# A 31-tap convolution as block-Toeplitz matmuls, LayerNorm sums on VectorE, and a mixer reordered by channel block, in a two-layer trunk on eight cores

## The chip, the cores and the metric

The kernel runs on the eight cores of one Trainium2 chip, two dies of four cores. Each core does the same work on its own 4096 tokens of 1024 channels. The metric is the device time of the slowest core. An execution falls into a fast state, or into a slow one in which the cores of one die, sometimes of both, show a lower granted TensorE clock and take longer. Stage times come from core 0 unless another core is named.

## The reference

Layer 0 is the part that changes. Its input projection feeds two mixers, whose outputs share one output projection:

```python
z = h @ w_in                                              # 1024 -> 2560
a_val, a_gate, b_gate, c_gate, b_val = jnp.split(z, [512, 1024, 1536, 2048], axis=-1)
a = a_val * jax.nn.sigmoid(a_gate)
a = causal_depthwise_conv(a, conv_a_w) + conv_a_b         # mixer A: 31 taps, 512 channels
a = jax.nn.silu(layer_norm(a, ln_a_g, ln_a_b))            # over the 512 channels
bo = b_gate * causal_depthwise_conv(c_gate * b_val, conv_b_w)   # mixer B: 3 taps
return jnp.concatenate([a, bo], axis=-1) @ w_out
```

A squared-ReLU MLP (1024 to 4096 and back) follows. Layer 1 has a chunked spatial gating mixer ("mixer 1" below) and another MLP. RMSNorm stands before each, and once more at the end.

## The kernel before

A core takes its tokens in four tiles of 1024 and runs mixer 0, MLP 0, mixer 1 and MLP 1 on each. The weights stream in pieces of 1 MB through a ring of four slots; GpSimd issues the next piece when TensorE has read an old one for the last time. SyncE issues everything else, in order.

Mixer A convolves with one diagonal matrix per tap and channel block; the matmuls use one entry in 128 of each matrix:

```python
for k in range(31):                       # for each of 4 blocks of 128 channels
    dg[j] = identf * w[:, k]              # built on VectorE
    e.matmul(banks[cb0], lhsT=dg[j], rhs=ab[:, k:k + 512], start=(k == 0), stop=(k == 30))
    e.matmul(banks[cb1], lhsT=dg[j], rhs=ab[:, 512 + k:1024 + k], ...)
```

LayerNorm's sums over channels are fp32 matmuls with a matrix of ones, 16 a tile. Mixer B then projects all c and v columns, and after them all b columns.

The last normalization multiplies into an output buffer, writes it out and loads the next tile's input behind it:

```python
small("dve", ... out=obuf[tb], in0=h[:, tb, :] ..., writes [("TT", "obuf", tb)])
P.op("sp", lambda e: e.dma_start(out=dst, in_=obuf[tb]), reads=[("TT", "obuf", tb)], dma="out")
if mt + 1 < n_mt:
    load_x(mt + 1, tb)
```

The name after `dma=` is the counter that the transfer increments. A later user of the same memory waits for that counter, and the helper always asks for its newest value, whichever transfer it was recorded for:

```python
if isinstance(s, tuple):       # a transfer's counter
    p = snap[s[1]]             # as many as have been issued by now
```

Between stages a "fence" folds all that is recorded for a memory region into one set, which every later write into the region waits for.

## Time and profile before

| what | us |
|---|---|
| three runs | 3658.84, 3241.15, 3693.83 |
| span of core 0 in the profiled run (fast) | 3245.0 |
| mixer 0 with its output projection, tiles 1 to 4 | 193.0, 194.2, 193.6, 191.2 |
| mixer 1, all tiles | 472.5 |
| both MLPs, all tiles | 1804.9 |
| before the first projection matmul | 44.5 |
| joints after tiles 1, 2, 3 | 30.0, 52.5, 50.8 |
| after the last matmul | 17.6 |

A stage begins with its first matmul and ends with the next stage's first; a joint runs from a tile's last matmul to the next tile's first projection matmul. The prediction below shows the views that this is read from.

### The profile page before, as it was taken

Reading aid. Unit: us, or ns where it says so; the run is one execution under the profiler, and the core shown is the slowest. Engines: PE = TensorE matmul, PEld = TensorE weight load, DVE = VectorE, ACT = ScalarE, POOL = GpSimd, SP = SyncE. Lnnn points to the kernel's source line nnn. Section 1 sums busy time; section 2 is a strip of 40 time slices with the busy share of each in tenths; the row PEclk is TensorE's granted clock in tenths of the full one; section 3 lists DMA queues with packets and bytes.
Section 4 is the critical chain, followed back from the end, with each engine's and each line's share of the span. In section 5 each row is a group of like instructions: output and inputs, shape, how many; then the busy total and the mean of one; then the engine's idle time right before and its main releaser. Section 6 shows DMA issues by size and latency. Waiting matters only on the chain.

```text
span 3245.0 us, 42214 instructions; the slowest of 8 cores (3232.0 to 3245.0 us)
## 1 busy us (share of the span) xinstructions
PE 2907.4 (90%) x13664; PEld 1346.0 (41%) x13936; DVE 1165.6 (36%) x2236; ACT 963.4 (30%) x1721; POOL 822.8 (25%) x865
## 2 busy tenths in 40 slices
PE   5989997999788999799779899979976989997997
PEld 3434443444334444344334344434433434443443
DVE  3461235313454214512245521451224452145123
ACT  2142145222223115521222411552122231155212
POOL 1004223342002331342200233134320023313432
PEclk9999998999899999899879999989987999998999
DMA  6235453466315453465811445335471144533542
GB/s 131 27 50 81 65 78 53 61 84 128 68 27 72 72 78 53 62 82 66 147 36 26 69 75 78 53 53 88 68 139 44 27 67 77 78 53 53 86 71 78
DMA packets 197205, 227.23 MB, mean 70 GB/s; under 512 B 3968, under 2 KB 188416, under 8 KB 196864
## 3 DMA queue, kind: packets, MB, share of 16 engines
q0 software_dynamic: 187200, 188.76, 41.1%
q1 hardware_dynamic: 9792, 35.76, 3.4%
q8 instruction: 118, 1.93, 0.2%
q14 instruction: 95, 0.78, 0.1%
HBM read 396.47 MB, written 16.78 MB: 127 GB/s over the span
## 4 chain that ended last, share of the span: by engine, by line
PE 76%; DVE 7%; issue 6%; DMA 5%; ACT 4%; POOL 1%; DVEq 0%; SPq 0%; ACTq 0%; POOLq 0%
PE bank L584 34%; PE bank L595 32%; PE bank L680 3%; PE bank L679 3%; DMA y<-TT 3%; PE bank L441 2%; DMA ring<-ev_w_out 1%; DVE TT L549 1%; POOL R L861 1%; DMA h<-x 1%; ACT R L810 1%; PE bank L707 1%; PE bank L700 1%; DVE TT L731 1%; ACT TT L806 1%
## 5 line engine op out<-in xcount | busy, mean ns | idle before, releaser
L584 PE MATMUL bank<-xnT,ring 128*128 128x512 bf16 x5756 | 1301.9, 385 | 57.3 <-ACT TT L756 22.1
L595 PE MATMUL bank<-ring,R 128*128 128x512 bf16 x5008 | 1132.0, 384 | 25.1 <-DVE R L782 11.2
L602 DVE TENSOR_TENSOR h<-bank,h 128x512 f32<-128x512 f32 x640 | 439.5, 691 | 1423.9 <-PE bank L595 1423.9
L584 PEld LDWEIGHTS bank<-xnT,ring 128*128 128x128 bf16 x5888 | 580.5, 99 | 767.8 <-issue 100.9
L595 PEld LDWEIGHTS bank<-ring,R 128*128 128x128 bf16 x5120 | 503.5, 99 | 627.0 <-issue 48.6
L621 ACT ACTIVATE TT<-bank 128x512 f32<-128x512 f32 x512 | 305.4, 597 | 1239.3 <-PE bank L584 1215.3
L623 POOL TENSOR_TENSOR R<-TT 128x512 bf16<-128x512 f32 x512 | 532.1, 1039 | 382.6 <-ACT TT L621 381.9
L441 PE MATMUL bank<-ident,xn_tm 128*128 128x128 bf16 x1024 | 90.4, 243 | 166.2 <-ACT st L454 98.9
L388 ACT ACTIVATE junk<-h 128x1024 bf16<-128x1024 f32 x160 | 167.0, 1044 | 134.3 <-DVE h L602 127.3
L679 PE MATMUL bank<-TT,dg 128*128 128x512 bf16 x480 | 181.2, 378 | 17.7 <-DVE dg L674 14.8
L680 PE MATMUL bank<-TT,dg 128*128 128x512 bf16 x496 | 188.5, 380 | 0.9
L298 POOL DMA_DIRECT2D ring<-w_0 x64 | 57.5, 898 | 444.9 <-PE bank L595 428.9
L298 POOL DMA_DIRECT2D ring<-w_1 x64 | 57.8, 903 | 441.4 <-PE bank L595 352.2
L426 ACT ACTIVATE xn_tm<-h,st 128x1024 bf16<-128x1024 f32 x112 | 128.2, 1144 | 127.6 <-DVE st L485 108.5
L444 DVE TENSOR_TENSOR xnT<-bank,sm 128x1024 bf16<-128x1024 bf16 x128 | 155.1, 1219 | 28.0 <-PE bank L441 26.7
L441 PEld LDWEIGHTS bank<-ident,xn_tm 128*128 128x128 bf16 x1024 | 74.6, 109 | 194.2 <-issue 178.1
L674 DVE TENSOR_SCALAR dg<-identf,sm 128x128 bf16<-128x128 f32 x496 | 133.7, 294 | 54.4 <-PE bank L680 5.0
L595 PE MATMUL bank<-ring,xnT 128*128 128x512 bf16 x500 | 114.3, 390 | 1.0 <-issue 0.4
L858 DVE TENSOR_TENSOR TT<-TT,biasT 128x512 f32<-128x512 f32 x64 | 71.7, 1154 | 80.0 <-ACT TT L849 76.7
L861 POOL TENSOR_TENSOR R<-TT,R 128x512 bf16<-128x512 f32 x64 | 95.9, 1532 | 8.2 <-ACT TT L849 5.2
L684 ACT ACTIVATE R<-bank,sm 128x512 f32<-128x512 f32 x32 | 22.0, 687 | 243.3 <-PE bank L680 241.8
L763 POOL COPY halo_c<-TT 128x2 f32<-128x2 f32 x16 | 6.0, 378 | 336.0 <-DVE TT L758 336.0
(84 smaller groups left out, 1159.3 us busy)
## 6 DMA issues: line engine op xcount, KB each, us to landing
ring<-w_0 POOLq DMA_DIRECT2D x64, 1024.0 KB, 11.5
ring<-w_1 POOLq DMA_DIRECT2D x64, 1024.0 KB, 11.9
ring<-ev_w_in POOLq DMA_DIRECT2D x20, 1024.0 KB, 14.0
h<-x SPq DMA_DIRECT2D x32, 512.0 KB, 7.1
ring<-od_w_in POOLq DMA_DIRECT2D x16, 1024.0 KB, 10.8
y<-TT SPq DMA_DIRECT2D x32, 512.0 KB, 3.7
ring<-ev_w_out POOLq DMA_DIRECT2D x8, 1024.0 KB, 13.6
ring<-od_w_out POOLq DMA_DIRECT2D x8, 1024.0 KB, 13.9
```

The costliest lines, as they stand in the source:

```text
L388: small("act", lambda e: e.activation(out=junk[jb][:], in_=h[:, tb, :], func=AF.Square, accum_out=st[:, c0 + tb:c0 + tb + 1]), h_keys(tb), ...
L441: r = e.transpose(tbk[:, kc * 128:(kc + 1) * 128], xn_tm[xb][:, kc * 128:(kc + 1) * 128], ident[:])
L444: small("dve", lambda e: e.tensor_tensor(out=xnT[:, :, tb * 128:(tb + 1) * 128], in0=tbk.rearrange("p (k n) -> p k n", k=8), in1=sm[:, SM_ ...
L584: r = e.matmul(banks[b][:], lhsT=ring[slot][:, kc, m * 128:(m + 1) * 128], rhs=xnT[:, kc, s * 512:(s + 1) * 512], start=(kc == 0), stop=(k ...
L595: r = e.matmul(banks[b][:], lhsT=lhs(kc, tb), rhs=ring[slot][:, kc, :], start=(kc == 0), stop=(kc == 7))
L602: small("dve", lambda e: e.tensor_tensor(out=h[:, tb, d * 512:(d + 1) * 512], in0=banks[b][:], in1=h[:, tb, d * 512:(d + 1) * 512], op=ALU ...
L621: small("act", lambda e, b=b, rb=rb: e.activation(out=rbuf[rb], in_=banks[b][:], func=AF.Relu), [("ps", b)], [("TT", "rbuf", rb)])
L623: small("pool", lambda e, rb=rb, hq=hq, c=j * 4 + m, s=s: e.tensor_tensor(out=hq[:, c, s * 512:(s + 1) * 512], in0=rbuf[rb], in1=rbuf[rb], ...
L674: small("dve", lambda e, j=j, m=m, k=k: e.tensor_scalar(out=dg[j][:], in0=identf[:], scalar1=sm[:, SM_CA + m * 31 + k:SM_CA + m * 31 + k + 1],
L679: e.matmul(banks[cb0][:], lhsT=dg[j][:], rhs=ab[:, k:k + 512], start=(k == 0), stop=(k == 30))
L680: return e.matmul(banks[cb1][:], lhsT=dg[j][:], rhs=ab[:, 512 + k:1024 + k], start=(k == 0), stop=(k == 30))
L861: small("pool", lambda e, hb=hb, sv3=sv3, tb=tb: e.tensor_tensor(out=yT[:, hb * 4:hb * 4 + 4, tb * 128:(tb + 1) * 128], in0=sv3, in1=uT[:, ...
```

## The change

The change means to take work from TensorE. Channels are cut into 16 groups of 32, and four token phases (token number modulo 4) are laid beside them, so that 128 rows hold 32 channels in four phases. One 128 by 128 block-Toeplitz matrix then does up to 16 products of tap and phase per channel, and nine lags replace 31 taps. The projection does not leave its result in that layout, so each block of 128 channels goes out to DRAM and comes back re-laid, and the normalized result goes through DRAM again on its way back ("hops"). The core of the diff:

```diff
-for k in range(31):                       # 248 matmuls of 512 columns a tile, 31 diagonals a block
-    dg[j] = identf * w[:, k]; matmul(cb0, dg[j], ab[:, k:k+512]); matmul(cb1, ...)
+for half_ in range(2):                    # 144 matmuls of 256 columns a tile, cw built once
+    g = 2 * gp + half_
+    for L in range(NLAG):                 # 9 lags
+        r = e.matmul(banks[b][:, half_ * TP:(half_ + 1) * TP], lhsT=cw[:, g, L * 128:(L + 1) * 128],
+                     rhs=A4.v[:, g, HB - L:HB - L + TP], start=(L == 0), stop=(L == NLAG - 1))
+# a_glu(m): the hop, on the sync queue
+P.op("sp", dma_start(out=scr_a[m] (4 phases), in_=ab), dma=f"a{m}")
+P.op("sp", dma_start(out=A4[4m:4m+4], in_=scr_a[m]), reads=[("scra", m)], dma=f"b{m}")
-mm1 / sums of squares: 16 fp32 matmuls with ones_f
+acc_s += pair; acc_q += pair * pair       # VectorE and ScalarE, under the convolution
+matmul(b, lhsT=blk, rhs=comb)             # one small matmul, within mixer B
+lazy(m, "pool", subtract mean); lazy(m, "dve", multiply by rstd); ScalarE Silu;
+lazy(m + 1, "sp", write scr_s[m]); lazy(m + 1, "sp", read back into mixT, two halves)
-mixer B: c and v columns of all blocks, then b columns of all blocks
+B_COLS = [c0, v0, c1, v1, b0, c2, v2, b1, c3, v3, b2, b3]; b_mix(m); b_gate(m - 1); b_release(min(m, 2))
-obuf: 8 buffers in region TT, all on counter "out", fenced between stages
+obuf: 4 buffers tracked by address, counters "out0" to "out3"
-x, y: rows tb * 128 to tb * 128 + 127 of a tile
+x, y: every fourth row of 512 (phase order)
-sm and cst loaded first, on counter "c"
+sm first, then x, then wexp and cst, all three on counter "c"
```

(The diff also moves the scratch tiles into one region tracked in steps of 256 bytes, and reorders the spatial weights to match the token order.)

## The prediction

> **Which time is meant.** The three runs before took 3658.84, 3241.15 and 3693.83 us: one fast, two slow. The profile fell in a fast run (its span is 3245.0 us), so I work from 3241 us and predict the fast state of the changed kernel.
>
> **What bounds the kernel now.** First the view of the cores, to know the state: both dies agree within 0.1%, so this is an undisturbed run.
>
> ```profile
> core 0: 3245.0 us, clock 0.957
> die 0 (median of its cores): 3236.5 us, clock 0.954
> die 1 (median of its cores): 3234.9 us, clock 0.958
> ```
>
> Next the page's chain of waits. TensorE is 76% of what ended last; the rest is not matmul, and that remainder is where waits hide. L584 and L595 are the plain projections, which the change leaves alone; L679 and L680 (the 31 taps) are 3% each; "DMA y<-TT 3%" is a surprise, since an output write should lie beside other work.
>
> ```profile
> PE 76%; DVE 7%; issue 6%; DMA 5%; ACT 4%; POOL 1%; DVEq 0%; SPq 0%; ACTq 0%; POOLq 0%
> PE bank L584 34%; PE bank L595 32%; PE bank L680 3%; PE bank L679 3%; DMA y<-TT 3%; PE bank L441 2%; DMA ring<-ev_w_out 1%; DVE TT L549 1%; POOL R L861 1%; DMA h<-x 1%; ACT R L810 1%; PE bank L707 1%; PE bank L700 1%; DVE TT L731 1%; ACT TT L806 1%
> ```
>
> Then I cut core 0 into stretches; the boundaries are where TensorE's line changes in the timeline. Each of the core's four tiles of 1024 tokens goes through the same stages. Tile 2's mixer 0 is three of the stretches below: mixer A with its convolution (837 to 926), the LayerNorm sums (926 to 941), and mixer B up to the start of the output projection (941 to 999). The row from 1322 is the spatial part of mixer 1. The last three are joints: the end of tile 1, the end of tile 2, and the end of the kernel. Read the length against PE busy.
>
> ```profile
> core 0: us, PE busy (x) PEld busy (x) DVE busy (x) ACT busy (x) POOL busy (x), PEclk, DMA share, GB/s
> 837.40:926.60 89.20, 82.66 (x368) 36.48 (x375) 39.86 (x133) 11.69 (x18) 3.51 (x10) 0.99 0.18 24
> 926.60:941.10 14.50, 14.45 (x32) 5.85 (x34) 2.08 (x3) 4.68 (x8) 0.00 (x0) 1.00 0.01 1
> 941.10:999.50 58.40, 47.41 (x197) 20.33 (x201) 43.70 (x52) 16.78 (x22) 5.32 (x10) 0.91 0.18 22
> 1322.30:1335.40 13.10, 5.53 (x65) 4.57 (x65) 10.62 (x13) 6.17 (x21) 10.20 (x8) 0.71 1.15 166
> 807.60:837.40 29.80, 8.10 (x64) 6.42 (x66) 18.12 (x37) 15.73 (x33) 1.08 (x2) 0.58 0.99 216
> 1598.60:1651.10 52.50, 8.13 (x66) 6.44 (x67) 21.96 (x45) 18.27 (x38) 1.00 (x2) 0.52 0.61 146
> 3213.00:3245.00 32.00, 14.31 (x65) 6.37 (x65) 15.74 (x30) 7.37 (x18) 0.00 (x0) 0.80 0.32 131
> ```
>
> Mixer A and the sums are bound by TensorE. Mixer B is not: its work is 192 matmuls, 41.5 us, in 58.4 us. And the joint after tile 2 costs 52.5 us where that after tile 1 costs 29.8.
>
> Last, the chain in time order, in mixer B, at the joint after tile 2, and at the end. TensorE sits before the output projection until the last piece of its weights lands; at the joint and at the end each final multiply waits for the output write before it.
>
> ```profile
> 986.79 12.34 DMA ring<-ev_w_out
> ```
>
> ```profile
> 1599.22 9.69 DMA y<-TT
> 1610.36 8.71 DMA y<-TT
> ```
>
> ```profile
> 3238.08 2.61 DMA y<-TT
> ```
>
> The source says why. All output writes share one counter, and the output buffers lie in a region that is fenced between stages, so after the first tile a write into any of them waits for every output write issued so far.
>
> The durations I use:
>
> ```profile
> L680 PE MATMUL bank<-TT,dg 128*128 128x512 bf16 x496 | 188.5, 380 | 0.9
> L700 PE MATMUL bank<-R,ones_f 128*128 128x512 f32 x64 | 29.1, 597 | 6.8 <-ACT R L684 6.8
> L731 DVE RECIPROCAL TT<-TT 128x512 f32<-128x512 f32 x8 | 26.8, 3353 | 14.8 <-ACT TT L729 14.8
> L858 DVE TENSOR_TENSOR TT<-TT,biasT 128x512 f32<-128x512 f32 x64 | 71.7, 1154 | 80.0 <-ACT TT L849 76.7
> L861 POOL TENSOR_TENSOR R<-TT,R 128x512 bf16<-128x512 f32 x64 | 95.9, 1532 | 8.2 <-ACT TT L849 5.2
> ```
>
> A matmul's 380 ns is latency; in a run of them, one starts every 0.216 us (16 in 3.45 us in the chain).
>
> **What the Trainium skill says.** "TensorE: Matmul & The Clock Gate", section "Wait — 56ns, not 53.3ns?": a warm matmul of N columns starts N/2.4 GHz plus about 2.5 ns after the last. The trace agrees at 512 columns (0.216 us) and at 128 (eight transposes in 0.45 us, 56 ns each, so a weight load hides behind even 128 columns). For 256 columns, which this trace lacks, that gives an estimate of 109 ns. The same page, "Seeing it yourself", reports a peak-current limit that takes a die to 13/16 of its clock with several cores busy; no fast run shows it, and I take it as a candidate for the slow state only. "DMA: Bandwidth & Descriptors", "Anatomy of one DMA": about 2 us fixed plus the bytes; the trace's 2.61 us for a 512 KB write at a quiet time agrees roughly. "SBUF — State Buffer", "Who interferes with whom": a VectorE operation with two SBUF inputs and a GpSimd operation that reads SBUF block each other; L858 at 1.15 us, where it took 0.69 us with GpSimd idle, agrees.
>
> **The change, part by part, per tile.**
>
> Mixer A. Before: 16 projection groups of 8 matmuls (128 x 0.216 = 27.6 us) plus 4 blocks x 31 taps x 2 halves = 248 matmuls, 53.6 us; the other 8 us of 89.2 are waits and a cold start. After: channels are cut into 16 groups of 32, four token phases fill the 128 rows, and 9 lags do the 31 taps: 16 x 9 = 144 matmuls of 256 columns, 144 x 0.109 = 15.7 us. The 496 diagonal builds on VectorE go too, but they lay beside TensorE. New: each of four channel blocks goes through DRAM, a 256 KB write and a 256 KB read in 512-byte pieces, on the one sync queue. Estimate 4 to 7 us a hop, since a weight piece is loading at the same time. All four gated projections come first, so block 3's data comes about 2 + 12 us after the 27.6 us, and TensorE meets it after six of eight convolution pairs, 11.8 us later: a wait of 0 to 7, take 3.5 us. With 1.5 us of cold start: 27.6 + 15.7 + 5 = 48.3 us. Saved: 41 us.
>
> LayerNorm sums. 16 fp32 matmuls (14.5 us) become one of 0.9 us inside mixer B, with VectorE adds under the convolution: about 1.4 us of adds and 1.5 us of ScalarE per pair of 2.0 us, so they keep up. Saved: 14.5 us.
>
> Mixer B. Work 41.5 + 0.9 us. The columns ordered by block release the first B piece mid-way, so the second ev_w_out piece is asked for some 17 us into B, not near its end; landing takes 13.6 us in the page, so the 12 us wait goes. VectorE after: per block 2 products, 3 taps and 2 gates about 6.6 us (from 0.69, 0.75 and 1.28 us rows), LayerNorm 4 x 1.3 us, one reciprocal of half the size (1.7 us) and some 3 us of small ones: about 40 us, starting 3.5 us late, so it finishes about 1 to 4 us after TensorE. The normalized rows go back through DRAM, four times write and read; I have the last land 41 us in, about when it is needed. Take 3.5 us of waiting: 45.9 us. Saved: 12.5 us.
>
> Together 68 us a tile, 272 us over four tiles.
>
> Joints. The new output buffers are tracked by address with one counter per buffer, so the chain through "DMA y<-TT" goes, though the description doesn't say so. Joints after tiles 2 and 3 fall from 52.5 and 50.8 (the same stretch a tile later) to about 29.8 us: 44 us. The end falls from 32 to about 10 us: 22 us.
>
> Start. The first projection matmul is at 44.5 us; 2 MB of constants no longer stand ahead of x in the queue. Save 8 us.
>
> Mixer 1. Tokens lie in another order, so the first output block needs four spatial chunks and not one. GpSimd makes one in two steps of 1.53 us; eight are done about 13 us after the first began, 3 us later than the projection starts today, but VectorE holds that projection up anyway 15 us later. Cost 2 us a tile: 8 us.
>
> Sum: 272 + 66 + 8 - 8 = 338 us; 3241 - 338 = 2903, say 2905 us.
>
> **Rivals.** First, the DRAM hops take the place of what was removed: eight hops a tile share one queue, and each read holds the queue until its write has landed. For it: 256 and 512-byte pieces, weight traffic with a DMA share near 1 at the joint. Against: mixers A and B use only 0.18 of the DMA. If a hop takes 10 us, TensorE waits 10 to 15 us more a tile: 2960 us. Second, VectorE becomes the bound in mixer B (43.7 of 58.4 us busy now, and GpSimd subtracts beside it): 5 us more a tile, 2925 us. Third, the joints don't fall because x loads bound them: 2950 us. On the other side, if neither re-layout nor VectorE shows at all, 7 us a tile come back: 2877 us.
>
> **Range and chances.** The rivals add up one by one, seldom all: 2845 to 2990 us. Even all three together (3041 us) is over 2% faster, so faster 0.97, same 0.02, slower 0.01.
>
> **What would show it.** Right: in mixer 0, from first projection matmul to output projection, 92 to 97 us where it is 162 now; 144 convolution matmuls a tile at 0.109 us; no "ring<-ev_w_out" and no "y<-" in the chain; joints near 30 us. Wrong: TensorE idle before the convolution's last pairs or before the output projection, ended by DMA; joints still at 50 us; or 256-column matmuls starting slower than 0.12 us apart.

## The result, and the profile after

The changed kernel is correct. Its six runs have a median of 2994.27 us (2955.62 to 3431.36), but three of them are slow: the fast ones are 2955.62, 2964.41 and 2968.08. The ratio to before is 0.9142, with a 95% interval of 0.9095 to 0.9189. (A ratio is the mean time of one kernel's fast runs over that of the other's in the same rounds, so it is not quite the ratio of the medians.) A control run of the same kernel later gave 2974.07 in the median of its fast runs, ratio 0.9169. So the fast state is some 280 us faster than before and about 60 us slower than the predicted 2905.

The profiled run has a disturbed die. The view of the cores shows which to read:

```profile
core 0: 2959.2 us, clock 0.964
...
die 0 (median of its cores): 2953.7 us, clock 0.964
die 1 (median of its cores): 3007.5 us, clock 0.944
```

Die 0 has the clock of a fast run, so core 0 is compared with core 0 of before. The disturbed cores show stretches at 0.81 of the clock: core 5, of die 1, had a mean of 0.81 between 60 and 190 us, core 0 of 0.96 in the same stretch, and no core of die 0 has a record at that level. These are its stretches, with the columns of the prediction's table: the start, the joint after tile 1, then mixer A and mixer B of tile 2, and the end.

```profile
0.00:51.40 51.40, 7.89 (x65) 6.27 (x66) 16.60 (x32) 15.80 (x29) 23.02 (x25) 1.00 0.66 150
761.80:794.40 32.60, 7.93 (x65) 6.26 (x65) 17.90 (x36) 16.24 (x34) 1.71 (x2) 0.58 0.90 204
794.40:839.60 45.20, 45.20 (x275) 27.12 (x274) 14.56 (x21) 16.35 (x30) 2.27 (x3) 0.96 0.47 94
839.60:889.80 50.20, 44.50 (x197) 19.44 (x195) 43.04 (x58) 16.74 (x30) 12.40 (x7) 0.97 0.46 86
2949.70:2959.20 9.50, 0.04 (x1) 0.00 (x0) 5.07 (x9) 1.75 (x6) 0.00 (x0) 0.61 0.52 212
```

The start and the end of the kernel before, cut at the same events:

```profile
0.00:44.50 44.50, 11.84 (x80) 9.89 (x82) 16.03 (x32) 15.80 (x29) 7.70 (x18) 1.00 1.02 216
3227.40:3245.00 17.60, 0.02 (x1) 0.00 (x0) 6.92 (x12) 2.69 (x7) 0.00 (x0) 0.64 0.32 132
```

Three readings. Mixer A is now 45.2 us with TensorE busy throughout; it was 103.7 with the sums. Mixer B still leaves TensorE idle for 5.7 of its 50.2 us (it was 58.4). And the end of before was 17.6 us long, counted from the last matmul, not the 32 that the prediction's last stretch suggests: that stretch began at 3213.00, and had 14.31 us of matmuls in it.

TensorE's timeline in tile 2 (start, duration, instruction, count; the bracket gives the idle time before it and what ended it) shows what mixer 0 consists of now:

```profile
794.40 29.57 PE L617 MATMUL bank<-xnT,ring 128*128 128x512 bf16 x128
823.81 15.94 PE L720 MATMUL bank<-Z,cw 128*128 128x256 bf16 x144
...
865.12 7.03 PE L617 MATMUL bank<-xnT,ring 128*128 128x512 bf16 x24 [2.07 <-DVE Z L823]
872.74 13.97 PE L617 MATMUL bank<-xnT,ring 128*128 128x512 bf16 x64 [0.60 <-DVE Z L847]
889.75 15.44 PE L628 MATMUL bank<-ring,Z 128*128 128x512 bf16 x63 [3.03 <-DVE Z L847]
```

The 144 convolution matmuls start 15.94 / 144 = 0.111 us apart. They follow the projection with no wait, and every wait in mixer B of this tile is ended by VectorE. The second hop is close behind: in the trace its last read landed at 889.32 us, 0.43 us before the output projection began. The account over all tiles of core 0:

| term | predicted saving | measured | difference |
|---|---|---|---|
| mixer 0 and output projection | 272 | 772.0 - 527.4 = 244.6 | -27 |
| joints after tiles 1 to 3 | 44 | 133.3 - 100.2 = 33.1 | -11 |
| end | 22 | 17.6 - 9.5 = 8.1 | -14 |
| start | 8 | 44.5 - 51.4 = -6.9 | -15 |
| mixer 1 and MLPs | -8 | 2277.4 - 2270.7 = 6.7 | +15 |
| sum | 338 | 285.6 | -52 |

By tile, mixer 0 with its output projection is 141.7, 129.7, 126.5 and 129.4 us: saved are 51 us in tile 1 and 62 to 67 in the others, where the prediction had 68 in each.

### The profile page after: what moved, and what is told of

It reads as the page before. It is cut to its first block, busy times and chain, and to the rows that moved or that the text cites. A ratio compares the mean times of both kernels' runs of the same rounds, so it can differ in the third digit from the quotient of the medians.

```text
span 3018.8 us, 39817 instructions; the slowest of 8 cores (2942.1 to 3018.8 us)
## 1 busy us (share of the span) xinstructions
PE 2752.6 (91%) x13148; PEld 1299.0 (43%) x13400; DVE 1068.3 (35%) x1813; ACT 964.6 (32%) x1773; POOL 871.7 (29%) x839
## 4 chain that ended last, share of the span: by engine, by line
PE 78%; DMA 6%; issue 6%; DVE 5%; ACT 3%; POOL 1%; SPq 0%; DVEq 0%; ACTq 0%; POOLq 0%
PE bank L628 39%; PE bank L617 36%; DMA scr_a<-Z 2%; PE bank L472 2%; DMA h<-x 2%; DMA scr_s<-Z 1%; PE bank L720 1%; ACT Z L894 1%; DMA cst<-bigc 1%; ACT Z L891 1%; POOL Z L957 1%; DVE Z L838 1%; DVE Z L888 1%; DMA Z<-scr_a 1%; DVE Z L954 0%
## 5 line engine op out<-in xcount | busy, mean ns | idle before, releaser
L617 PE MATMUL bank<-xnT,ring 128*128 128x512 bf16 x5760 | 1327.3, 390 | 42.7 <-ACT Z L971 12.0
L628 PE MATMUL bank<-ring,Z 128*128 128x512 bf16 x5008 | 1152.5, 389 | 31.5 <-DVE Z L954 13.8
L628 PEld LDWEIGHTS bank<-ring,Z 128*128 128x128 bf16 x5120 | 507.8, 100 | 648.9 <-issue 137.7
L664 ACT ACTIVATE Z<-bank 128x512 f32<-128x512 f32 x512 | 305.5, 597 | 1279.9 <-PE bank L617 1261.1
L666 POOL TENSOR_TENSOR Z<-Z 128x512 bf16<-128x512 f32 x512 | 531.8, 1039 | 399.0 <-ACT Z L664 398.4
L484 DVE TENSOR_TENSOR xnT<-bank,sm 128x1024 bf16<-128x1024 bf16 x96 | 116.4, 1220 | 38.5 <-PE bank L472 23.8
L954 DVE TENSOR_TENSOR Z<-Z,biasT 128x512 f32<-128x512 f32 x64 | 71.9, 1157 | 81.2 <-ACT Z L945 77.9
L957 POOL TENSOR_TENSOR Z<-Z 128x512 bf16<-128x512 f32 x64 | 95.9, 1531 | 8.7 <-ACT Z L945 5.7
L628 PEld LDWEIGHTS bank<-ring,xnT 128*128 128x128 bf16 x512 | 51.0, 101 | 68.0 <-issue 16.0
L720 PE MATMUL bank<-Z,cw 128*128 128x256 bf16 x576 | 70.1, 287 | 7.4 <-DMA Z<-scr_a 7.4
L909 POOL TENSOR_TENSOR st<-st,mhalf 128x1 f32<-128x1 f32 x32 | 17.6, 550 | 183.6 <-DVE st L907 183.6
L720 PEld LDWEIGHTS bank<-Z,cw 128*128 128x128 bf16 x576 | 59.0, 103 | 18.8 <-issue 8.5
```

The source lines that it names most:

```text
L484: small("dve", lambda e: e.tensor_tensor(out=xnT[:, :, tb * 128:(tb + 1) * 128], in0=tbk.rearrange("p (k n) -> p k n", k=8), in1=gcol.unsq ...
L617: r = e.matmul(banks[b][:], lhsT=ring[slot][:, kc, m * 128:(m + 1) * 128], rhs=xnT[:, kc, s * 512:(s + 1) * 512], start=(kc == 0), stop=(k ...
L628: r = e.matmul(banks[b][:], lhsT=lhs(kc, tb), rhs=ring[slot][:, kc, :], start=(kc == 0), stop=(kc == 7))
L664: small("act", lambda e, b=b, rb=rb: e.activation(out=rb.v, in_=banks[b][:], func=AF.Relu), [("ps", b)], rb.k())
L666: small("pool", lambda e, rb=rb, hq=hq, c=c, s=s: e.tensor_tensor(out=hq.v[:, c, s * 512:(s + 1) * 512], in0=rb.v, in1=rb.v, op=ALU.mult), ...
L720: r = e.matmul(banks[b][:, half_ * TP:(half_ + 1) * TP], lhsT=cw[:, g, L * 128:(L + 1) * 128], rhs=A4.v[:, g, HB - L:HB - L + TP], start=( ...
```

## The experiments

Eighteen kernels ran. "Mixer 0" below is the sum of its four tiles without the output projection, as the mean of the eight cores of the profiled run: 626.6 us before, 395.4 in the control of the changed kernel. (That is some 156 us a tile before, where the prediction says 162: the output projection's first matmuls came before its wait for the last weight piece, and a stage ends here with the next one's first matmul.)

### What each part of the change is worth

**Nine of 31 taps in the kernel before** (wrong result), which takes away about the TensorE work that the Toeplitz form takes away. The diagonals of the other taps, built on VectorE, go with them; the layout, LayerNorm and mixer B stay.

```diff
-for k in range(31):
+for k in range(9):
```

> The kernel before with 9 of its 31 taps (wrong result on purpose): as many matmul columns as the changed convolution has, with the old layout, old LayerNorm and old order of mixer B. If the convolution was bound by TensorE, each tile loses 176 matmuls of 0.217 us = 38 us, 153 us in all, ratio 0.953. If the gated products or VectorE bound that stage (rival), less than 100 us go, ratio 0.97 or more.

Fast runs of 3087 to 3090 us, ratio 0.9518 [0.9501, 0.9534]; mixer 0 fell from 625.6 to 472.3 on core 1. So 153 us of TensorE time in the convolution come off the total one for one. The new form's 144 matmuls of 0.111 us cost about what 72 of the old ones of 0.216 us would (15.9 and 15.6 us), and 72 is nine taps.

**LayerNorm sums back on TensorE, in the changed kernel.**

```diff
-acc_s / acc_q on VectorE, one matmul of comb
+for g in range(16): matmul(b, lhsT=blk, rhs=a_conv[g]); per pair: square on ScalarE, 2 matmuls
```

> The changed kernel with the LayerNorm sums back on TensorE: 32 fp32 matmuls of 256 columns after the convolution and no adds on VectorE. If the sums lay on the path, each tile gains 13.8 us of matmul and 1.7 us of waiting for ScalarE and loses the 0.9 us matmul: 14.6 us, 58 us in all, ratio to before 0.932. If VectorE, relieved of the adds, gives some of it back in mixer B (rival), 30 to 45 us.

Correct, ratio 0.9351 [0.9328, 0.9375]. Mixer 0 rises by 59 us, to 454.5, as the prediction's 14.5 us a tile have it. The ratio says 68 us for the whole kernel against 0.9142 and 59 against the control's 0.9169; each interval is some 15 to 30 us wide.

**Mixer B's columns and weight releases in the old order, in the changed kernel.**

```diff
-B_COLS = [c0, v0, c1, v1, b0, c2, ...]; per block: b_mix, b_gate, b_release
+B_COLS = [c0..c3, v0..v3, b0..b3]; all b_mix, then release, then all b_gate
```

> The changed kernel with mixer B's columns and releases in the old order: all products first, all gates last, the two B pieces released after the last product. The prediction's view is that this brings back the 12 us wait for the second piece of ev_w_out in every tile: 48 us, ratio to before 0.929. The rival is that the piece, asked for 13.8 us before the projection and landing in 9 to 14 us, costs 0 to 5 us a tile, 0 to 20 us in all, since VectorE's lag in mixer B hides it.

Correct. Only one run was fast, 2999.01 us, against 2956 to 2975 for the changed kernel; that profile shows mixer 0 at 420.4 and the output projection 5 us longer in all. The order is worth some 30 us, which is neither the 48 of the prediction's view nor the 0 to 20 of the rival. In this run all 32 tiles of the eight cores wait before the output projection for the second hop, 12 to 17 us. The chain on core 1 (start, duration, what) shows how it costs now:

```profile
881.10 12.83 DMA scr_s<-Z
```

One 256 KB write into DRAM takes 12.83 us while a weight piece loads. In the kernel before it was the weight piece itself that TensorE waited for.

### The joints and the end

**Own counter per output buffer in the kernel before.** The prediction named the shared counter as the cause of the long joints.

```diff
-reads=[("TT", "obuf", tb)], dma="out")
+reads=[("TT", "obuf", tb)], dma=f"out{tb}")
```

> The kernel before with one thing changed: each of the eight output buffers has its own transfer counter. If the serial output writes alone made the second and third joints longer than the first, those two fall from 52.5 and 50.8 to about 30 us and the stretch after the last matmul from 17.6 to about 10 us: 43 + 8 = 51 us off, a ratio of 0.984. If the x loads bound the joints (rival), they stay near 45 us and at most 15 us go, ratio 0.995 or more.

A miss: the one fast run took 3241.45 us, and on an undisturbed core (4) the joints were 29.8, 51.5 and 50.7. The chain still goes through the writes, as in this one:

```profile
1598.75 7.78 DMA y<-TT
```

The fence folds all eight counters into one set, and the helper asks for each one's newest value, so a multiply still waits for the write just issued.

**The same, and the wait asks for the recorded write.**

```diff
-p = snap[s[1]]
+if not s[1].startswith("out"):
+    p = snap[s[1]]
```

> The kernel before with its own counter per output buffer, as the first such run, and in addition a wait for an output write asks only for the write that the fence recorded, not for all writes issued by now. The first such run left the joints at 51.5 and 50.7 us, since the fence joins all eight counters and the wait took each one's newest value. If that is the cause, the second and third joints now fall to 30 to 34 us and the stretch after the last matmul from 17.6 to about 10 us: 45 us, ratio 0.986. If x loads bound the joints, they stay at 45 us or more.

One fast run, 3195.5 us, and a fast profile. The stretch that was 52.5 us is now, on core 1:

```profile
1596.10:1626.40 30.30, 7.89 (x64) 6.25 (x65) 17.90 (x36) 15.90 (x34) 1.00 (x2) 0.57 1.01 214
```

Joints are 29.2, 30.3 and 29.4, and the end 9.3: 98 us, where core 1 of the kernel before has 147 (core 0 has 151), and the time is some 50 us lower. That confirms the serial writes, and it says that a separate counter alone is not the repair: the wait must ask for the write that it needs. The changed kernel gets there by tracking the buffers by address.

**Contiguous rows of x and y in the changed kernel** (wrong result). Its joints were 32.6, 34.1 and 33.5 us, not 30. The loads of x land later than before (the page's issue rows: transfers, size of each, median us to landing; first before, then after):

```profile
h<-x SPq DMA_DIRECT2D x32, 512.0 KB, 7.1
```

```profile
h<-x SPq DMA_DIRECT2D x32, 512.0 KB, 12.5
```

```diff
-rows r0 + j, r0 + j + 4, ... of 512
+rows r0 + j * 128 to r0 + j * 128 + 127
```

> The changed kernel with x and the output moved in blocks of 128 consecutive rows, as before, and not every fourth row (wrong result on purpose). The joints are 32 to 34 us where the kernel before with its output counters mended has 29 to 30, and x takes 12 us to land where it took 7. If the row stride makes the transfers slower, the three joints fall to about 30 us and the median landing of x to 7 us: 9 us off. If the traffic of the held weight pieces does it (rival), nothing changes.

Joints on core 0 fall to 28.3, 30.3 and 29.6, with x at 9.6 us; in the mean of eight cores three joints take 88.7 us, and 97.3 in the control. So the strided rows cost about 3 us a joint. The total barely moves (0.9117 [0.9074, 0.9159]).

### The start

**Own counters for the two late constants in the changed kernel.** The chain of the start waits for them, though nothing needs them for long:

```profile
8.47 23.67 DMA cst<-bigc
```

VectorE's first normalization reads the small parameters, which landed first, but their counter is shared with a 1 MB transfer behind the whole of x, and the helper asks for its newest value.

```diff
-writes=wexp.k(), dma="c")          -writes=[("cst",)], dma="c")
+writes=wexp.k(), dma="cw")         +writes=[("cst",)], dma="cc")
```

> The changed kernel with the convolution's weights and the constants on counters of their own, so that a wait for the small parameters no longer waits for the 1 MB of constants queued after x. If that shared counter is why the first projection starts at 51 us, it starts at 36 to 40 us: 11 to 15 us off, ratio to before about 0.910. If the x loads or the norm chain bound the start (rival), it moves by less than 4 us.

Correct. The chain of core 1 now begins with x itself:

```profile
2.92 13.53 DMA h<-x
```

The first projection matmul comes at 37 to 41 us instead of 50.5 to 52.4, in spite of a profile that is slow on both dies. The fast runs, 2961.49 and 2964.22, are hardly better than without it: ratio 0.9112 [0.9039, 0.9185]. A gain of 12 us (0.4%) is inside the interval, so these runs alone do not settle what the start is worth. The Trainium skill, "DMA: Bandwidth & Descriptors", section "Why a DMA increments its semaphore by 16 and not by 1", advises "One semaphore per in-flight slot, not one per stream" for correctness. The start shows what sharing costs in time: with a shared counter this program waits for the newest transfer, 23.67 us.

### What binds mixer 0

**No first hop** (wrong result): VectorE writes the convolution's input directly, in the wrong layout.

```diff
-out=ab (phases); write scr_a[m]; read A4[4m:4m+4]
+out=A4[4m:4m+4, ...]
```

> The changed kernel with the gated product written straight into the convolution's input, without the write and read through DRAM (wrong result on purpose). The trace shows TensorE waiting for these hops 5.9 us in tile 1 and 0 to 1.4 us in the others. If that is all they cost, 6 to 10 us go, ratio 0.911 to 0.912. If they also slow other transfers or VectorE (rival), 20 us or more.

Ratio 0.9095 [0.9023, 0.9168]. The waits within the convolution are gone. Tile 1 takes 96.9 us in the mean of eight cores, 7 us less than the control: there the start-up weights and constants travel beside the hop. The other three together are 6 us shorter than in the control (3 us shorter than in the changed kernel's first profile, which has 288.3 for them). The first hop costs some 1 to 2 us in an ordinary tile.

**No second hop** (wrong result): Silu writes the mixed rows directly.

```diff
-out=S4[g] ... write scr_s[m]; read mixT in two halves
+out=mixT[m, (g % 4) * TP : ...]
```

> The changed kernel with the normalized rows written straight into the output projection's input, without the second trip through DRAM (wrong result on purpose). If these hops are what TensorE waits for before the projection, the projection starts 7 us earlier in tile 1 and 1 to 3 us in the others: 10 to 16 us, ratio about 0.910. If VectorE's lag in mixer B is what it waits for (rival), tiles 2 to 4 don't move and only the 7 us of tile 1 go.

Ratio 0.9119 [0.9046, 0.9193]; tiles 2 to 4 of core 0 stay at 95.2, 93.8 and 95.2, and mixer 0 falls by 8 us in the mean of eight cores, to 387.0. Every wait before the output projection is now ended by VectorE. So in most tiles VectorE's lag sets the end of mixer B, and the hop lies beside it.

The trace shows why VectorE lags. These are two of its operations in mixer B of tile 2 and GpSimd's subtractions of the mean (GpSimd's line covers three of them; the second and third VectorE lines are the multiplication by one over the standard deviation, on the first and the second block):

```profile
846.47 7.33 POOL L779 TENSOR_TENSOR Z<-Z 128x1024 f32<-128x1024 f32 x3 [10.68 <-DVE Z L764]
846.56 2.53 DVE L768 TENSOR_TENSOR Z<-Z 128x256 f32<-128x256 f32 x1
...
855.69 4.06 DVE L779 TENSOR_TENSOR Z<-Z 128x1024 f32<-128x1024 f32 x1
...
864.89 1.22 DVE L779 TENSOR_TENSOR Z<-Z 128x1024 f32<-128x1024 f32 x1
```

An operation on 256 elements takes 2.53 us when it starts beside a subtraction; its neighbours of that size, which read PSUM (where TensorE puts its sums) and not SBUF (the working memory on the chip), take 0.41 and 0.42. The multiply takes 4.06 on the first block and 1.22 on the second. The slow ones have two SBUF inputs, and so has the subtraction: it is the blocking that the prediction cited, here at three to six times the duration.

**Subtractions on VectorE.**

```diff
-("pool", ln_mean, ALU.subtract)
+("dve", ln_mean, ALU.subtract)
```

> The changed kernel with the four mean subtractions a tile on VectorE and not on GpSimd. VectorE gets 4 x 1.2 us more work a tile, and loses about 7 us of blocked time (2.1 + 2.0 + 2.8 in the trace). If blocking is the cause, mixer B gets 1 to 3 us a tile shorter although VectorE does more; if only VectorE's amount of work counts (rival), it gets 4 to 5 us a tile longer.

Ratio 0.9195 [0.9167, 0.9222], mixer 0 at 401.4: not faster. The waits inside mixer B fall from 3.8 us a tile in the control to 1.7, and in their place 14 of 32 tiles wait 11 to 14 us before the output projection, for the read of the second hop.

**LayerNorm's short operations with one SBUF input each.**

```diff
-ln_t = ps * (1/512); rstd = mean * mean; ln_t = (ln_t + eps) - rstd       # VectorE
+rstd = Square(mean)                                                      # ScalarE
+ln_t = ps * (1/512) - rstd                                               # VectorE, from PSUM
```

> The changed kernel with the two short LayerNorm operations that took 2.5 and 2.4 us each (two SBUF inputs, beside GpSimd's subtractions) made so that VectorE has one SBUF input: the square moves to ScalarE, the difference reads PSUM. If blocking by GpSimd makes VectorE late in mixer B, VectorE's chain is 4 us shorter and so is mixer B, 3 to 4 us a tile, 12 to 16 us in all, ratio to before about 0.909. If something else sets mixer B's end (rival), less than 4 us go.

Correct, ratio 0.9162 [0.9123, 0.9202]: no gain. The square is on ScalarE now, and the difference, which took 2.38 us with two SBUF inputs, takes 0.42 (tile 2 of core 4):

```profile
838.75 0.42 DVE L769 SCALAR_TENSOR_TENSOR Z<-bank,Z 128x256 f32<-128x256 f32 x1 [0.62 <-ACT Z L768]
```

The waits inside mixer B fall from 3.8 to 1.9 us a tile, and the same new wait appears: 17 of 32 tiles wait between 4 and 14 us before the output projection, for the hop.

So a quicker VectorE uncovered another wait. Is it the hop, and why is it late? Four kernels went together on one chip.

**The control**, the changed kernel once more.

> Control: the changed kernel unaltered, beside the other three on one chip. Both theories expect what was measured first: ratio about 0.914, fast runs 2955 to 2968, the waits before the out projection in tiles 2 to 4 about 1 us and ended by a VectorE instruction.

Fast runs 2973.85 to 2975.21, ratio 0.9169 [0.9149, 0.919], mixer 0 at 395.4. The expectation about the waits held in part: of 15 tiles (2 to 4 of cores 0 to 4) ten wait 3 us or less, but four wait 4 to 11 us for the hop, so the hop shows now and then in the changed kernel itself.

**The short operations and no second hop** (wrong result).

> LayerNorm's short operations with one SBUF input (which made VectorE quicker but won nothing), and the second hop through DRAM taken away (wrong result on purpose). If the second hop ate the gain of the quicker VectorE: waits before the out projection at most 3 us in every tile, mixer 0 at 91 to 93 us a tile, 12 to 20 us below the control. If something else ate it (the tile is bound by TensorE itself in mixer B): the waits go but the tiles stay at 94 to 95 us and the time within 5 us of the control.

Ratio 0.9108 [0.9077, 0.914]; mixer 0 at 377.3, 18 us below the control, and in no tile of the eight cores is the wait before the output projection over 2.6 us. The hop is what ate the gain.

**The short operations, and the release of a w1 weight piece (of MLP 0, which comes next) moved behind the last gate.**

```diff
-b_release(min(m, 2))      # after each gate
+b_release(1)              # the rest after b_gate(3)
```

> LayerNorm's short operations with one SBUF input, and the release of the w1 weight piece moved from after the second block to after the last gate, so that no weight piece travels beside the second hops. If the weight pieces delay the hops: the 4 to 10 us waits before the out projection fall below 3 us and the ratio to about 0.909. If the hops are late for another reason (their own issue and landing, after the last gates): the waits stay at 4 to 10 us and the ratio at 0.914 to 0.917.

Ratio 0.9162 [0.9135, 0.9188], mixer 0 394.0, waits as before. This told nothing about the pieces, because they did not move: GpSimd has no other work at that place, reaches the later release early, and issues the piece as soon as TensorE has read the old one. In the trace of core 4 the piece went out at 867.61, right before the third block's hop at 869.94.

**The short operations, and the w1 pieces issued only when all four hops have landed.**

```diff
-b_release(3)
+b_release(3, mixT.k(0, 4 * T))    # the issue also waits for the reads into mixT
```

> The release in the previous attempt was moved in the program, but GpSimd's queue reached it early and the w piece still went out beside the third hop (issued 867.6, hop written 869.9 to 879.4). Here both w1 pieces are issued only once all four second hops have landed. If weight pieces delay the hops: the last hop lands 3 to 5 us after its issue as the others do, waits before the out projection at most 3 us in nearly every tile, mixer 0 at 376 to 384, 12 to 20 us below the control's 2952 to 2974, ratio about 0.910. If the hops are late by themselves: waits of 9 to 11 us stay in half of the tiles, mixer 0 at 383 to 403 and ratio 0.914 to 0.917.

Correct, ratio 0.9114 [0.9096, 0.9132], fast runs 2948 to 2956, mixer 0 at 377.2: the same as without the second hop. No tile of any core waits over 2.8 us before the output projection. (This run and the last combination below came later, on another chip, beside runs of the kernel before on that chip; the fast ones took 3239 to 3243 us there, and 3242 to 3245 beside the control.) Compare tile 2 of core 4 in the timelines, first with the short operations alone, then with the pieces held. Each hop is a write (scr_s<-Z), and SyncE issues its read (Z<-scr_s) when the write has landed:

```profile
860.61 0.92 POOL L334 DMA_DIRECT2D ring<-w  x1 [10.14 <-PE bank L619]
...
862.73 0.60 SPq L786 DMA_DIRECT2D scr_s<-Z  x1
871.62 0.91 SPq L790 DMA_DIRECT2D Z<-scr_s  x2
...
886.05 16.82 PE L630 MATMUL bank<-ring,Z 128*128 128x512 bf16 x64 [10.75 <-DMA Z<-scr_s]
```

```profile
864.24 0.40 SPq L786 DMA_DIRECT2D scr_s<-Z  x1
866.68 0.91 SPq L790 DMA_DIRECT2D Z<-scr_s  x2
...
874.59 0.92 POOL L334 DMA_DIRECT2D ring<-w  x1 [22.49 <-DMA Z<-scr_s]
...
879.62 15.66 PE L630 MATMUL bank<-ring,Z 128*128 128x512 bf16 x64 [2.70 <-DVE Z L847]
```

The write of 256 KB takes 871.62 - 862.73 = 8.9 us beside a weight piece of 1 MB issued 2 us earlier, and 2.4 us when the piece waits. As the queue is in order, the fourth hop starts late too. The Trainium skill, "DMA: Bandwidth & Descriptors", section "Queues, rings and completion order", says that each DMA engine takes turns between the queues it has work for, a packet at a time. A small transfer then pays for its neighbour's packets. The trace agrees that it pays; that turns by packet are the way it comes about, no run here shows. Nor do the runs separate a core's own weight piece from those of the other cores, which were held in the same run.

The six kernels side by side, as means of eight cores:

| changed kernel with | tile 1 of mixer 0 | tiles 2 to 4 together | mixer 0 |
|---|---|---|---|
| nothing else (control) | 104.1 | 291.3 | 395.4 |
| no second hop | 100.9 | 286.1 | 387.0 |
| quicker VectorE | 101.2 | 293.8 | 395.0 |
| quicker VectorE, no second hop | 98.3 | 279.0 | 377.3 |
| quicker VectorE, release moved in the program | 101.3 | 292.7 | 394.0 |
| quicker VectorE, issue of the w1 pieces held | 97.5 | 279.7 | 377.2 |

Taking away one of the two limits gives 8 or 0 us; taking away both gives 18. One more row is needed to judge the 8: in the changed kernel's first profile the undisturbed die has 389.3 in the mean of its four cores, 6 us below the control. So 8 us are hardly more than two profiles of one kernel differ by, and 18 us are well beyond it.

### The repairs together

**Own counters, short operations, first tap of mixer B's convolution on ScalarE, and the two late start-up pieces issued right behind x.**

> The changed kernel with the counters split, the LayerNorm operations of one SBUF input, the first of the three taps of mixer B on ScalarE, and the third and fourth weight pieces asked for as soon as x has landed. 12 us off at the start, 4 to 10 us in tile 1's hops, 4 x 4 to 7 us in mixer B: 32 to 50 us less than the changed kernel, about 2920 us, ratio to before 0.898 to 0.904.

Correct, ratio 0.9175 [0.9149, 0.92]: nothing won. The start falls to 35 to 38 us, and mixer 0 rises to 400.1 (385 to 423 by core), with waits of up to 16.5 us for the hop. The mean span over the cores is 2955 us, 5 below that of the quicker VectorE alone (2960), but the slowest core decides: it took 2980.8, with 419.3 in mixer 0.

**The same, with the moved release above, and at a joint the held weight pieces only when the last block of x has landed.**

```diff
-release(held.pop(0))
+issue(held.pop(0) + NSLOT, extra=h_keys(NTB - 1))
```

> All the repairs at once: own counters for the late constants, one SBUF input in the short LayerNorm operations, the first tap on ScalarE, the w1 piece released after the last gate, and at a joint the next held weight pieces only after the last block of x has landed. If weight pieces beside short transfers are what costs: start 38 us, no long wait before the out projection, joints at 30 us or below, 2915 to 2930, ratio about 0.90. If not: start 38 us and the rest as in the previous combination, ratio 0.914 to 0.918.

Correct, ratio 0.9087 [0.9038, 0.9135]. The joints fall to 26 to 27 us on every core, but mixer 0 is at 400.6, since the release again did not move. Why the joints fall shows on TensorE's third row of transposes, which waits for a block of x, after tile 2. First the changed kernel, then the next experiment, which has the same joint:

```profile
1514.28 1.01 PE L472 MATMUL bank<-ident,xn_tm 128*128 128x128 bf16 x8 [10.97 <-ACT st L498]
```

```profile
1476.92 1.01 PE L474 MATMUL bank<-ident,xn_tm 128*128 128x128 bf16 x8 [2.84 <-ACT st L500]
```

**The same, with the issue of the w1 pieces really held.**

> All the repairs with this same hold of the w1 pieces. If weight pieces delay the hops: mixer 0 at 376 to 386 with start 37 and joints 26 kept, spans of 2910 to 2925 on every core, ratio about 0.898. If not: as the previous combination, 2942 to 2957, ratio about 0.909.

Correct. Fast runs 2924.65 to 2936.84, ratio 0.9039 [0.9016, 0.9061], and none of the four runs was slow. Start 35 to 38, joints 26 to 28, mixer 0 at 383.0, spans 2914 to 2924. That is 1.4% below the control (0.9169), whose interval lies well clear of it, and the best of all kernels here. The spans are as expected, the ratio a little above: with the first tap on ScalarE, TensorE waits 4.7 us for VectorE at the end of mixer B in most tiles, where the version without the move waits 0.9 to 2.8 us. In tile 2 of core 4 VectorE itself now sits idle 1.50, 2.44 and 0.72 us until ScalarE has made the first tap. That move is probably a loss of some 6 us (383.0 against 377.2); it was not run alone.

## Why the prediction was right or wrong

Right were the direction, the mechanism of the savings in the convolution, the sums and the joints, and most sizes. The convolution's matmuls start 0.111 us apart (0.109 estimated), mixer A takes 45.2 us (48.3), the sums are worth 59 us in four tiles (58), no weight piece and no output write is on the path of core 0's tile 2, and that tile's mixer 0 takes 95.3 us, within the 92 to 97 named. The fast runs, 2956 to 2968, lie within the range of 2845 to 2990. The median of all six runs, 2994.27, does not, as three of them were slow.

What failed are sizes in the sum: 338 us of savings were forecast and 285.6 came on core 0, in five terms. The largest is the first, "272 us over four tiles" in mixer 0, which measured 244.6; the start is the one term whose wait was wrong too.

- **Mixer 0, "together 68 us a tile".** It measured 51 in tile 1 and 62 to 67 in the others. The step that failed is taking tile 2 for all four: in tile 1 both hops run beside the start-up transfers. There TensorE waited 5.9 us at the convolution and 7.3 us before the output projection, both ended by a hop's read. That is 17 of the 27 us, and the first rival in small, in one tile of four. In mixer B the sum "about 40 us" of VectorE left out the blocking that the prediction itself had cited. (Its parts as listed, 4 x 6.6 + 4 x 1.3 + 1.7 + 3, come to 36.3 and not to 40; with the 2.1 + 2.0 + 2.8 us that the trace shows as blocked they reach 43.2.) It measured 43.0 us busy in a stretch of 50.2, where 45.9 were predicted. The second rival (VectorE as the bound) is what tiles 2 to 4 show, with the first close behind it: take VectorE's lag away and the hops, delayed by weight pieces, take its place; with both gone 18 us come back.
- **Joints, "about 29.8 us".** The cause, serial output writes, is confirmed by the kernel before with only that repaired. The step's detail is not: an own counter per buffer did nothing by itself. The size was missed by some 4 us a joint, of which about 3 are x in strided rows, which the prediction did not cost.
- **The end, "from 32 to about 10 us".** It did fall to 9.5, but from 17.6. The 32 us were a stretch that began 14 us before the last matmul.
- **The start, "save 8 us".** It cost 6.9. The reasoning looked at the order of the transfers and not at their counters: the small parameters kept the counter that is now shared with 1 MB behind x. With its own counter the start does fall, to 37 to 41 us.
- **Mixer 1, "cost 2 us a tile".** It was not slower at all (470.1 after 472.5). The prediction had given the reason itself, that VectorE holds the projection up anyway, and charged the 8 us all the same.

The prediction's third rival, joints bound by x, holds for the last few microseconds only: joints fell to 26 us when the weight pieces kept clear of x. Its figure for all three rivals together, 3041 us, is a slip: 55, 20 and 45 us over 2905 make 3025. Nothing hangs on it. Its candidate for the slow state, a clock of 13/16, gets support: the disturbed cores show that level (0.81), and no core of a fast profile does. What sets it off stays open.

Two things stay open. Holding the w1 pieces without the quicker VectorE was not run; judging by the kernel without the second hop it would give at most 8 us, an estimate. And fast runs of the same kernel on different occasions differ (2964 and 2974 in the median), which is of the size of several effects here.

## What to carry to other kernels

When a change routes data through DRAM on the critical path, look at what else the DMA engines carry at that moment, and hold back a large prefetch that isn't needed yet until the small transfer has landed; put that wait on the issue itself, as a release moved in program order may be reached just as early. When a repair of one engine gives nothing, read what now ends the wait in the same place before giving the repair up: two near-equal waits must go together. And give each transfer that something waits for its own counter, and check that the wait asks for that transfer and not for the newest one.

## What the Trainium skill lacked or had wrong

- "DMA: Bandwidth & Descriptors", "Queues, rings and completion order", has no figure for a small transfer beside a large one of another queue. Here a write of 256 KB took 2.4 us with no weight piece in flight, and 8.9 us (once 12.8) beside one or two weight pieces of 1 MB.
- The same page, "Why a DMA increments its semaphore by 16 and not by 1", gives only correctness as the reason for separate semaphores. A shared one cost about 12 us at the start here (51.5 us in the control, 39.0 with own counters, in the mean of eight cores), and waiting for the newest output write cost 50 us.
- The same page has no figure for a load of rows that are four rows apart (its row-pitch figures begin at 512 KiB): 512 KB in rows of 4 KB landed 11.3 to 12.5 us after issue, and 9.6 us with contiguous rows in the same kernel. Weight pieces in flight matter more: with these held back, the strided rows landed in 7.0 us.
- "TensorE: Matmul & The Clock Gate", "Seeing it yourself", has a die fall to 13/16 once three cores run dense matmuls. In every fast run all eight cores did, at a mean granted clock of 0.94 to 0.97, and no fast profile has a record at 13/16. The level itself is there: the cores of a slow die have stretches at 0.81, and slow dies had means from 0.80 to 0.95.
- "SBUF — State Buffer", "Who interferes with whom", quotes a "DVE 6.8× slower" without the operation or its length. Here a VectorE operation on 256 elements took 2.38 us beside a GpSimd subtraction, and 0.42 us once one of its inputs came from PSUM.
